# A second weight pool, other rooms and steps in the feed-forward block of a two-layer trunk

## The chip, the cores and the metric

The kernel runs on one core of a Trainium2 chip. The metric is the device time of one execution in microseconds (us). The core has five engines that run side by side, each through its own instructions in order: TensorE (PE in the profile, with its weight loads as PEld), VectorE (DVE), ScalarE (ACT), GpSimd (POOL) and SyncE (SP, which here only issues transfers). POOL and ACT issue transfers too; all transfers share 16 DMA engines. Engines wait for each other through semaphores.

## The reference, cut to what matters

The model is a trunk of two layers. Layer 0 is a gated linear attention, layer 1 a chunked softmax attention; each is followed by the same kind of feed-forward block (FFN). The change touches the FFN alone.

```python
D_MODEL, SEQ, FFN_DIM, FFN_CONV = 1024, 1024, 2816, 3

def conv_ffn(xn, w_up, conv_w, conv_b, w_down):
    h = causal_dwconv(xn @ w_up, conv_w) + conv_b     # 1024 x 5632, three taps along the sequence
    gate, val = h[..., :FFN_DIM], h[..., FFN_DIM:]
    return (jax.nn.silu(gate) * val) @ w_down         # back to 1024 x 1024

h = h + conv_ffn(rmsnorm(h, f_norm[layer]), f_w_up[layer], f_conv[layer], f_conv_b[layer], f_w_down[layer])
```

All of it is float32.

## The kernel before, in words

**Products of float32.** An operand of a product is cut in two: a high part (a cast to the matmul's type, on ACT or POOL) and a low part (operand minus high part, on POOL or DVE). A product is the sum of high x high, high x low and low x high, so three matmuls for each pair of tiles (`triple`). The cuts of the up-weights are called `uh`, `ul`, those of the down-weights `dh`, `dl`, those of the hidden channels (the down-product's other operand) `eh`, `el`.

**Tiles.** The 2816 hidden channels are 22 tiles `j` of 128. Both large products use a scheme of Strassen's kind: seven products of half size in the place of eight, with sums and differences of quarters of the operands. `product(j, n)`, n = 1 to 7, is one of the seven of the up-product of tile j (its gate and its value together); `second(g, n)` is one of the seven of the down-product of the pair g of hidden tiles, g = 0 to 8 for tiles 0 to 17; its products run in the order n = 1, 2, 5, 3, 6, 7, 4. Each is 12 matmuls. Tile 0 is done by eight plain products (`plain`), and tiles 18 to 21 by plain products at the end (`part` in layer 0, `tile_of` in layer 1), for which their hidden values are kept as cut tiles `hid` (function `hidden`).

**Order.** All products of a layer stand in one list `seq`, one step each. Everything else is a job, put at a step with `at(step, function, rank)`; the loop at the end runs, for each step, its jobs in order of rank and then its product. So the order of the instructions on every engine is written out by hand. A steady group is 21 steps: 14 up-products (two tiles) and 7 down-products.

**What stands where.** `load` brings a quarter of an up-weight (256 KB) into a room `r11`, `r12`, `r21` or `r22`. Those of tile 0 are issued by POOL, all others by SP. `operand` makes the sum that product n needs (DVE) and cuts it (ACT, then POOL, or DVE). `load_a` and `weights` do the same for the down-weights, with rooms `a11` to `a22` and `ay`; `channels` makes the channels' operand and its cut `e`. `drain` moves a down-product from PSUM into a staging tile on ACT or DVE; `send` adds it, as a transfer that accumulates (512 KB, issued by POOL), to one of four quarters of h in memory, `d_r` or, in layer 1, `d_c`. The first of the seven, n = 1, belongs to all four quarters: it is summed over the groups in two halves `d_e`, and at the end each half is read back (`load_e`) and sent three more times (`send_e`).

**Rooms.** Weights and cuts of the FFN lie in one pool `wf` at the right end of the on-chip memory; a tile waits for the last access to whatever lay at its address. Before the FFN, the residual's norm (lines 353 to 391: squares on ACT, their sum `nacc` on DVE, two small products `pss` and `psb` on PE, the scaling of h on DVE) uses the other free space. Eight slots h0 to h7 of the pool `hp` (1024 x 128 values each) hold, in turn, the values of four tiles (`val`, slots j mod 4), four staging tiles (h4 to h7), `hid` and the shared sum's halves. In layer 1 the slots have names with another number, and are used alike.

**End.** `load_last` loads the down-weights of tiles 18 to 21 (`fr`, into rooms of `wf`), `cut_last` cuts them (`fh`, `fl`); `load_r` (layer 1) loads what is to be added (`res`).

The lines of the profile that matter below: L1357 is every sum, difference and low cut of the FFN (`tt`; tiles tell which), L1377 the high cuts, L1389 to L1391 the matmuls of both products (tiles `pu` and `pd`), L1435 the loads of up-weights, L1472 to L1478 the convolution's taps, L1492 `hid`'s high part, L1710 and L1718 the sends, L1714 `load_e`, L1758 and L1764 the last tiles' weights and their cut.

Of the kernel before, what the change touches and what calls it, by code (L numbers as in the profile page):

```python
# [9 lines left out]
F32 = mybir.dt.float32  # L10
F32R = mybir.dt.float32r
# [5 lines left out]
P = 128  # L17
SEQ = 1024
KT = 8
HALF = 512  # L20
NH_A = 8
NH_B = 16
FP = 22
# [5 lines left out]
def trunk_kernel(  # L29
# [15 lines left out]
    nc = tc.nc  # L45
    SB = dict(reuse_waits="tile")
# [300 lines left out]
    hp = wp = None  # L347
# [157 lines left out]
    with ExitStack() as ph:  # L505
# [709 lines left out]
        h, late = [], None  # L1215
# [136 lines left out]
    def ffn(layer, h, hp, xs, tail, d_r, last):  # L1352
# [3 lines left out]
        sub, add = ALU.subtract, ALU.add  # L1356
# [4 lines left out]
        left, right = ExitStack(), ExitStack()  # L1361
        tp = left.enter_context(tc.tile_pool(name=f"ft{layer}", bufs=1, **SB))
        wf = right.enter_context(tc.tile_pool(name=f"fw{layer}", bufs=1, side="right", **SB))
        ctx_x = ExitStack()
        xt = ctx_x.enter_context(tc.tile_pool(name=f"xt{layer}", bufs=1, **SB))
        NG = 9
        RINGS = dict(u=3, d=2, e=2)
# [3 lines left out]
        def at(i, f, rank=1):  # L1371

            jobs.setdefault(max(i, 0), []).append((rank, f))

        def cut_high(src, ring, copy=nc.scalar.copy):
            hi, lo = [wf.tile([P, HALF], F32R, name=ring + x, tag=ring + x, bufs=RINGS[ring]) for x in "hl"]
            copy(hi, src)  # L1377
            return hi, lo

        def cut_low(src, hi, lo, eng):  # L1380
            tt(eng, lo, src, hi.bitcast(F32), sub)
# [45 lines left out]

        def room(j, q):
            tag = {(2, 12): "dh", (1, 21): "a21", (1, 22): "a22"}.get((j, q), f"r{q}")
            return wf.tile([P, 4, P], F32, name=f"r{q}", tag=tag, bufs=1 if tag == "r12" or tag[0] == "a" else 2)  # L1430

        def load(j, q, t_=None):
            t_ = t_ or room(j, q)
# [22 lines left out]
        pre, conv_t, hid, keep, bank = {}, {}, {}, {}, {}  # L1456
# [26 lines left out]
        def hidden(j, c0=0, c1=SEQ):  # L1483

            if j not in hid:
                if j == FP - 1:
                    hid[j] = [fin.tile([P, SEQ], F32R, name=f"hid{i}", tag=f"hid{i}") for i in "hl"]
                else:
                    room_ = {18: 6, 19: 4, 20: 2}[j]
                    hid[j] = [hp.tile([P, SEQ], F32R, name=f"hid{i}", tag=f"h{layer + 1}_{room_ + n}") for n, i in enumerate("hl")]  # L1490
            (hh, hl), v_ = hid[j], conv_t[j, 1]
            nc.scalar.copy(hh[:, c0:c1], v_[:, c0:c1])  # L1492
            tt(nc.vector, hl[:, c0:c1], v_[:, c0:c1], hh[:, c0:c1].bitcast(F32), sub)
# [29 lines left out]
        pos = {}  # L1523
# [34 lines left out]
        for c, (j, n) in enumerate(plan):  # L1558
# [3 lines left out]
            for g in range(NG):  # L1562
                for n, o in zip(ORDER, (2, 3, 5, 6, 8, 9, 11) if g == 0 else (-2, 0, 2, 4, 6, 8, 10)):
                    if c == 7 * (2 * g + 1) + 6 + o:
                        step(("d", g, n), lambda g=g, n=n: second(g, n))
        end = pos[FP - 1, 7]
        early = pos["p", 1, 3]
        for i, (j, n) in due.items():
            if i < early:
                low = []  # L1570
# [7 lines left out]
        def nx(j, s):  # L1578
            return pos[j + 1, s] if j + 1 < FP else end + s
# [23 lines left out]
        for j in range(3, FP - 1):  # L1603
# [4 lines left out]
        when = {  # L1608
            0: [(11, (g0,), 0), (12, (v0,), 0), (13, (v1,), 2), (13, (v2,), 2.7), (15, (g1, g2, silu), 2), (17, (gated,), 2)],
            1: [(18, (v0, v1), 2), (19, (v2, g0), 2), (20, (g1,), 2), (21, (g2, silu), 2), (22, (gated,), 2)],  # L1610
            2: [(24, (v0, v1), 2), (25, (v2, g0), 2), (26, (g1,), 2), (27, (g2, silu), 2), (28, (gated,), 2)],
        }
        for j in range(3, FP - 1):
            when[j] = [(pos[j, 7], (v0, v1), 2), (nx(j, 1), (v2, g0), 2), (nx(j, 2), (g1,), 2), (nx(j, 3), (g2, silu), 2), (nx(j, 4), (gated,), 2)]
            if j >= 2 * NG:
                when[j].append(({18: pos["d", NG - 1, 4] + 3, 19: pos["d", NG - 1, 4] + 7}.get(j, nx(j, 5)), (hidden,), 1.9))
        for j, w_ in when.items():
            for i, fs, r in w_:
                at(i, lambda j=j, fs=fs: [taps(j, *f) if isinstance(f, tuple) else f(j) for f in fs], r)
# [27 lines left out]
        araw, aops, bops, banks, stage = {}, {}, {}, {}, {}  # L1647

        def load_a(g, q):
            araw[g, q] = wf.tile([P, HALF], F32, name=f"a{q}", tag=f"a{q}", bufs=1)  # L1650
            nc.sync.dma_start(out=araw[g, q], in_=w_dn[(2 * g + q % 10 - 1) * P : (2 * g + q % 10) * P, hs(q // 10 - 1)])

        def weights(g, n):
            a = lambda q: araw[g, q]
            if n == 5:
                araw[g, 0] = wf.tile([P, HALF], F32, name="ay", tag="ay", bufs=1)
                tt(nc.vector, a(0), a(21), a(22), add)
            elif n == 3:
                tt(nc.vector, a(0), a(0), a(11), sub)
                tt(nc.vector, a(12), a(12), a(0), sub)  # L1660
            elif n == 7:
                tt(nc.vector, a(21), a(11), a(21), sub)
            aops[g, n] = cut(a({1: 11, 2: 12, 5: 0, 3: 12, 6: 0, 7: 21, 4: 22}[n]), "d")

        def channels(g, n):
            b11, b12, b21, b22 = [conv_t[2 * g + k, 1][:, hs(s)] for k in range(2) for s in range(2)]
            if n == 5:
                tt(nc.vector, b11, b12, b11, sub)
            elif n == 6:
                tt(nc.vector, b11, b22, b11, sub)  # L1670
            elif n == 7:
                tt(nc.vector, b12, b22, b12, sub)
            elif n == 4:
                tt(nc.vector, b21, b21, b11, sub)
            src = {1: b11, 2: b21, 5: b11, 3: b22, 6: b11, 7: b12, 4: b21}[n]
            bops[g, n] = cut_high(src, "e")
            cut_low(src, *bops[g, n], nc.gpsimd if n in (3, 6, 7) else nc.vector)

        def second(g, n):
            new = n in (1, 5, 6)  # L1680
# [18 lines left out]
        def total(n, u):  # L1699
            if n == 1:  # L1700
                return d_e[u]
            c, s = where[n]
            return d_c[c, s, u]
# [6 lines left out]
                    nc.gpsimd.dma_start(out=total(n, u), in_=stage[g, n, u], accum_op=add)  # L1710

        def load_e(u):
            stage["e", u] = hp.tile([P, SEQ], F32, name="stage", tag=f"h{layer + 1}_{4 + u}")
            nc.sync.dma_start(out=stage["e", u], in_=d_e[u])  # L1714

        def send_e(n):
            for u in range(2):
                nc.gpsimd.dma_start(out=total(n, u), in_=stage["e", u], accum_op=add)  # L1718

        for g in range(NG):  # L1720
            p_ = {n: pos["d", g, n] for n in ORDER}
            b_ = {n: pos["d", g - 1, n] for n in ORDER} if g else {1: p_[1] - 4, 3: p_[1] - 4, 7: p_[1] - 4, 4: p_[1] - 3}
            for q, n in ((11, 7), (12, 3), (21, 7), (22, 4)):
                at(b_[n] - 2, lambda g=g, q=q: load_a(g, q), 3 + q / 100)
            for n in ORDER:
                at(p_[n] - 3, lambda g=g, n=n: weights(g, n), 1.2)
                at(p_[n] - 3, lambda g=g, n=n: channels(g, n), 1.4)
                at(p_[n] + 1, lambda g=g, n=n: drain(g, n), 0)
                if n not in (3, 5):
                    at(p_[n] + 2, lambda g=g, n=n: send(g, n), 0.5)  # L1730
        fin_at = pos["d", NG - 1, 4]
        for u in range(2):
            at(pos["d", NG - 1, 7] + 3, lambda u=u: load_e(u), 3)
        for n, i in ((6, 4), (7, 5), (4, 6)):
            at(fin_at + i, lambda n=n: send_e(n), 0.5)


        k0 = 2 * NG
# [8 lines left out]

        def load_last(q):
            tag = ("a11", "a12", "r11", "r21", "r22", "r11", "r22", "r21")[q]
            bufs = 1 if tag[0] == "a" else 2  # L1750
            if layer == 0:
                t_ = wf.tile([P, 4, P], F32, name="fr", tag=tag, bufs=bufs)
                nc.sync.dma_start(out=t_, in_=w_dn[k0 * P :, q * P : (q + 1) * P].rearrange("(k p) m -> p k m", p=P))
                t_ = t_.rearrange("p k m -> p (k m)")
            else:
                k, c = q // 2, q % 2
                t_ = wf.tile([P, HALF], F32, name="fr", tag=tag, bufs=bufs)
                nc.sync.dma_start(out=t_, in_=w_dn[(k0 + k) * P : (k0 + k + 1) * P, hs(c)])  # L1758
            fw[q] = t_

# [68 lines left out]
        else:  # L1829
# [6 lines left out]
            res = {}  # L1836

            def load_r(t):

                for c in range(2):  # L1840
                    if t < 4:
                        tag = ("eh", "el", "dh", "dl")[t % 2 * 2 + c]
                        r_ = wf.tile([P, 4, P], F32, name="res", tag=tag, bufs=2)
                    else:
                        r_ = actp.tile([P, 4, P], F32, name="res", tag=f"x{'hl'[c]}{t}_1")
                    for u in range(2):
                        nc.sync.dma_start(out=r_[:, 2 * u : 2 * u + 2], in_=d_r[c, t // 4, u].rearrange("p (f t) -> p f t", f=2)[:, :, kc[t % 4]])
                    res[t, c] = r_
# [79 lines left out]
    with ExitStack() as ph:  # L1928
# [204 lines left out]
        h = []  # L2133
# [163 lines left out]
```

## Time and profile before

| what | value |
|---|---|
| median of 3 runs | 2687.33 us (2683.79 to 2688.33) |
| profiled execution | 2685.01 us, of which span 2683.3 us |
| mean granted clock of TensorE | 0.981 |
| TensorE busy | 2542.1 us, 95% of the span |
| VectorE, ScalarE, GpSimd busy | 67%, 53%, 56% |
| transfers | 326.71 MB, mean 122 GB/s |
| first FFN | about 680 to 1375 us of the span |
| second FFN | about 1966 us to the end |

A group of instructions is named by its line, its engine and `out<-in` with the names of the tiles. In a view of waits, a line tells which engine and line waited for which, the total in us, how many times, and the longest. In a timeline a line has the start, the length, what ran, and in brackets the idle time before it and what ended that. The chain of waits follows the work that ended last backwards, from what released each piece. Matmuls overlap: one that is listed with 0.39 us is followed by the next after 0.23 us.

### The profile page before, as it was taken

The numbers are of one execution on the slowest core, as the hardware profiler recorded it, in microseconds if no ns is written. First come the engines' busy times: TensorE is split into PE (matmuls) and PEld (weight loads), VectorE is DVE, ScalarE is ACT, GpSimd is POOL, SyncE is SP. The second block draws the span as 40 slices with busy tenths as digits, with TensorE's granted clock in tenths as the row PEclk, the third lists the DMA queues.
The fourth block names the chain that finished last, engine by engine and source line by source line (L and its number), as shares of the span: only waits on it lengthen the run. The fifth ranks groups of instructions, "written<-read, shape, count | busy, mean of one in ns | idle before, by whom it ended". The sixth has DMA issues, their size and how long they took to land.

```text
span 2683.3 us, 39404 instructions
## 1 busy us (share of the span) xinstructions
PE 2542.1 (95%) x13933; PEld 2083.7 (78%) x13933; DVE 1807.4 (67%) x3084; ACT 1410.3 (53%) x2714; POOL 1492.2 (56%) x1490
## 2 busy tenths in 40 slices
PE   7999999999899999999899999998979999999988
PEld 5888778888677888788678888887766788888767
DVE  5756765553678777877676666665468777778856
ACT  5444546563455555555355555555345555555633
POOL 3655543346257777777545444434243777777851
PEclk9999999999899999999899999999989999999989
DMA  4534435455237777767831111114222577777685
GB/s 129 137 102 118 121 117 158 138 172 170 59 82 152 150 153 144 144 130 141 200 117 50 50 47 42 50 40 147 88 87 75 134 149 144 151 154 143 133 184 173
DMA packets 317845, 326.71 MB, mean 122 GB/s; under 512 B 33232, under 2 KB 240848, under 8 KB 317648
## 3 DMA queue, kind: packets, MB, share of 16 engines
q1 hardware_dynamic: 286192, 219.07, 27.7%
q0 software_dynamic: 26560, 96.48, 20.4%
q10 hardware_dynamic: 4896, 8.65, 0.9%
q8 instruction: 109, 1.79, 0.3%
q14 instruction: 88, 0.72, 0.1%
HBM read 180.94 MB, written 143.20 MB: 121 GB/s over the span
## 4 chain that ended last, share of the span: by engine, by line
PE 40%; issue 8%; DVE 8%; POOL 7%; ACT 3%; DMA 3%; ACTq 0%; DVEq 0%; POOLq 0%
PE pu L1391 5%; PE pu L1390 4%; PE pu L1389 4%; PE acc L120 3%; PE acc L121 3%; POOL ul L1357 3%; PE acc L122 3%; PE pd L1391 2%; PE pd L1390 2%; PE pd L1389 2%; DVE r L1357 2%; DVE val L1475 2%; PE ptp L2047 2%; PE poT L2077 1%; ACT uh L1377 1%
## 5 line engine op out<-in xcount | busy, mean ns | idle before, releaser
L1357 POOL TENSOR_TENSOR ul<-r,uh 128x512 fp32r<-128x512 f32 x282 | 440.2, 1571 | 354.4 <-ACT uh L1377 331.7
L120 PE MATMUL acc<-xh,whi 128*128 128x512 f32 x896 | 376.2, 420 | 0.3 <-ACT xh L1096 0.2
L1377 ACT CAST uh<-r 128x512 fp32r<-128x512 f32 x296 | 179.7, 620 | 365.3 <-DVE r L1357 289.2
L121 PE MATMUL acc<-xl,whi 128*128 128x512 f32 x896 | 354.6, 396 | 1.6 <-POOL xl L379 1.0
L122 PE MATMUL acc<-xh,wlo 128*128 128x512 f32 x896 | 353.7, 395 | 0.6 <-POOL wlo L105 0.6
L105 POOL TENSOR_TENSOR wlo<-wraw,whi 128x256 fp32r<-128x256 f32 (+1 forms) x293 | 236.0, 836 | 204.7 <-ACT whi L103 162.8
L1389 PE MATMUL pu<-xh,uh 128*128 128x512 f32 x552 | 219.7, 398 | 25.8 <-POOL uh L1377 17.2
L1391 PE MATMUL pu<-xh,ul 128*128 128x512 f32 x552 | 219.1, 397 | 7.1 <-POOL ul L1357 7.0
L1390 PE MATMUL pu<-xl,uh 128*128 128x512 f32 x552 | 218.5, 396 | 1.0 <-POOL xl L379 1.0
L122 PEld LDWEIGHTS acc<-xh,wlo 128*128 128x128 f32 x896 | 169.4, 189 | 38.5 <-POOL wlo L105 1.0
L121 PEld LDWEIGHTS acc<-xl,whi 128*128 128x128 f32 x896 | 170.8, 191 | 26.2 <-POOL xl L379 3.1
L1357 DVE TENSOR_TENSOR r<-r,r 128x512 f32<-128x512 f32 x168 | 178.0, 1059 | 19.2 <-POOL ul L1357 19.1
L120 PEld LDWEIGHTS acc<-xh,whi 128*128 128x128 f32 x896 | 170.7, 191 | 23.3 <-ACT xh L1096 1.2
L1475 DVE SCALAR_TENSOR_TENSOR val<-vpre,colt,val 128x1023 f32<-128x1023 f32 (+2 forms) x92 | 154.3, 1677 | 39.3 <-ACT val L1472 39.2
L1695 ACT COPY stage<-pd 128x1024 f32<-128x1024 f32 x180 | 173.2, 1012 | 1.1 <-PE pd L1391 1.0
L1357 POOL TENSOR_TENSOR dl<-a,dh 128x512 fp32r<-128x512 f32 x90 | 160.5, 1784 | 20.5 <-ACT dh L1377 20.5
L2027 POOL TENSOR_SCALAR sS<-sS,st 128x640 f32<-128x640 f32 (+4 forms) x128 | 87.6, 688 | 143.6 <-DVE st L2026 124.4
L1389 PEld LDWEIGHTS pu<-xh,uh 128*128 128x128 f32 x552 | 105.7, 191 | 49.9 <-POOL uh L1377 18.1
L1475 DVE SCALAR_TENSOR_TENSOR gate<-gpre,colt,gate 128x1023 f32<-128x1023 f32 (+2 forms) x92 | 134.4, 1461 | 0.2
L2025 ACT ACTIVATE sS<-sS,st 128x640 f32<-128x640 f32 (+4 forms) x128 | 89.1, 696 | 83.2 <-DVE st L2024 83.0
L1391 PEld LDWEIGHTS pu<-xh,ul 128*128 128x128 f32 x552 | 105.5, 191 | 33.3 <-POOL ul L1357 11.4
L1357 DVE TENSOR_TENSOR el<-val,eh 128x512 fp32r<-128x512 f32 x72 | 68.0, 945 | 90.5 <-ACT eh L1377 90.5
(389 smaller groups left out, 7109.4 us busy)
## 6 DMA issues: line engine op xcount, KB each, us to landing
r<-in_f_w_up_dram SPq DMA_DIRECT2D x168, 256.0 KB, 4.3
d_r<-stage POOLq DMA_DIRECT2D x78, 512.0 KB, 7.6
d_c<-stage POOLq DMA_DIRECT2D x70, 512.0 KB, 8.0
a<-in_f_w_down_dram SPq DMA_DIRECT2D x72, 256.0 KB, 2.8
wraw<-in_a_w_in_dram SPq DMA_DIRECT2D x32, 512.0 KB, 4.6
d_e<-stage POOLq DMA_DIRECT2D x32, 512.0 KB, 9.3
wraw<-in_a_w_out_dram SPq DMA_DIRECT2D x16, 512.0 KB, 4.1
d_r<-h ACTq DMA_DIRECT2D x32, 256.0 KB, 2.7
```

What stands on the lines that cost most here:

```text
L105: nc.gpsimd.tensor_tensor(lo[:, c], raw[:, c], hi[:, c].bitcast(F32), op=ALU.subtract)
L120: mm(ps, hi[:, kw, wcol : wcol + P], rh[k][s], start=st, stop=False)
L121: mm(ps, hi[:, kw, wcol : wcol + P], rl[k][s], start=False, stop=False)
L122: mm(ps, lo[:, kw, wcol : wcol + P], rh[k][s], start=False, stop=sp)
L1357: tt = lambda eng, o, a, b, op: eng.tensor_tensor(o, a, b, op=op)
L1377: copy(hi, src)
L1389: mm(ps, w[0][:, cw], x[0], start=first, stop=False, skip_group_check=True)
L1390: mm(ps, w[0][:, cw], x[1], start=False, stop=False, skip_group_check=True)
L1391: mm(ps, w[1][:, cw], x[0], start=False, stop=last, skip_group_check=True)
L1475: nc.vector.scalar_tensor_tensor(t_[:, a:c1], p_[:, a - step : c1 - step], w[:, 2 - step : 3 - step], t_[:, a:c1], op0=ALU.mult, op1=ALU.add)
L1695: nc.scalar.copy(t_, ps)
L2025: nc.scalar.activation(S, S, AF.Exp, bias=st[:, 1:2], accum_out=st[:, 2:3])
```

## The change

Four things are edited.

1. The down-product's weights (`a11` to `a22`, `ay`), the channels' cuts (`eh`, `el`) and, at the end, the tiles that take over their rooms go to a pool `wd` of their own, which lies below `wf` on the right. What stays in `wf` thereby lies at higher addresses.
2. The hidden tiles 18, 19 and 20 go to slots (h5, h6), (h7, h2) and (h3, h4) instead of (h6, h7), (h4, h5) and (h2, h3); tile 18 is cut two steps later.
3. The shared sum: the first half is read back into h3 at the step of the last group's product 5, and sent two and three steps after it; the second half into h4, two steps after the last down-product, and sent two and three steps after that. Before, both were read back at one step, into h4 and h5, and each send was issued for both halves.
4. The channels' high cut comes ahead of the weights' work of the same step, and the low cut one step later. Of the low cuts, POOL makes those of products 5, 6 and 7 (before: 3, 6 and 7) and DVE the others.

```diff
@@ ffn
+        wd = right.enter_context(tc.tile_pool(name=f"fd{layer}", bufs=1, side="right", **SB))
...
         def cut_high(src, ring, copy=nc.scalar.copy):
-            hi, lo = [wf.tile([P, HALF], F32R, name=ring + x, tag=ring + x, bufs=RINGS[ring]) for x in "hl"]
+            hi, lo = [(wd if ring == "e" else wf).tile([P, HALF], F32R, name=ring + x, tag=ring + x, bufs=RINGS[ring]) for x in "hl"]
...
         def room(j, q):
             tag = {(2, 12): "dh", (1, 21): "a21", (1, 22): "a22"}.get((j, q), f"r{q}")
-            return wf.tile([P, 4, P], F32, name=f"r{q}", tag=tag, bufs=1 if tag == "r12" or tag[0] == "a" else 2)
+            return (wd if tag[0] == "a" else wf).tile([P, 4, P], F32, name=f"r{q}", tag=tag, bufs=1 if tag == "r12" or tag[0] == "a" else 2)
...
-                    room_ = {18: 6, 19: 4, 20: 2}[j]
-                    hid[j] = [hp.tile([P, SEQ], F32R, name=f"hid{i}", tag=f"h{layer + 1}_{room_ + n}") for n, i in enumerate("hl")]
+                    room_ = {18: (5, 6), 19: (7, 2), 20: (3, 4)}[j]
+                    hid[j] = [hp.tile([P, SEQ], F32R, name=f"hid{i}", tag=f"h{layer + 1}_{n}") for n, i in zip(room_, "hl")]
...
-        end = pos[FP - 1, 7]
+        end, fin_at = pos[FP - 1, 7], pos["d", NG - 1, 4]
...
-                when[j].append(({18: pos["d", NG - 1, 4] + 3, 19: pos["d", NG - 1, 4] + 7}.get(j, nx(j, 5)), (hidden,), 1.9))
+                when[j].append(({18: fin_at + 5, 19: fin_at + 7}.get(j, max(nx(j, 5), fin_at + 9)), (hidden,), 1.9))
...
         def channels(g, n):
...
             bops[g, n] = cut_high(src, "e")
-            cut_low(src, *bops[g, n], nc.gpsimd if n in (3, 6, 7) else nc.vector)
+            return lambda: cut_low(src, *bops[g, n], nc.gpsimd if n in (5, 6, 7) else nc.vector)
...
         def load_e(u):
-            stage["e", u] = hp.tile([P, SEQ], F32, name="stage", tag=f"h{layer + 1}_{4 + u}")
+            stage["e", u] = hp.tile([P, SEQ], F32, name="stage", tag=f"h{layer + 1}_{(3, 4)[u]}")
             nc.sync.dma_start(out=stage["e", u], in_=d_e[u])
 
-        def send_e(n):
-            for u in range(2):
-                nc.gpsimd.dma_start(out=total(n, u), in_=stage["e", u], accum_op=add)
+        def send_e(u, n):
+            nc.gpsimd.dma_start(out=total(n, u), in_=stage["e", u], accum_op=add)
...
                 at(p_[n] - 3, lambda g=g, n=n: weights(g, n), 1.2)
-                at(p_[n] - 3, lambda g=g, n=n: channels(g, n), 1.4)
+                low = []
+                at(p_[n] - 3, lambda g=g, n=n, low=low: low.append(channels(g, n)), 1.1)
+                at(p_[n] - 2, lambda low=low: low[0](), 1.1)
...
-        fin_at = pos["d", NG - 1, 4]
-        for u in range(2):
-            at(pos["d", NG - 1, 7] + 3, lambda u=u: load_e(u), 3)
-        for n, i in ((6, 4), (7, 5), (4, 6)):
-            at(fin_at + i, lambda n=n: send_e(n), 0.5)
+        for u, i in ((0, pos["d", NG - 1, 5]), (1, fin_at + 2)):
+            at(i, lambda u=u: load_e(u), 3)
+            for k, n in enumerate((6, 7, 4)):
+                at(i + 2 + k // 2, lambda u=u, n=n: send_e(u, n), 0.6)
```

In the same way `load_a`, `weights` (for `ay`), `load_last` (where its room is an `a`) and `load_r` (where it is `eh` or `el`) take their tiles from `wd`.

More of the change, by code (lines that the diff above doesn't have):

```diff
@@ L1649, in load_a @@
         def load_a(g, q):
-            araw[g, q] = wf.tile([P, HALF], F32, name=f"a{q}", tag=f"a{q}", bufs=1)
+            araw[g, q] = wd.tile([P, HALF], F32, name=f"a{q}", tag=f"a{q}", bufs=1)
             nc.sync.dma_start(out=araw[g, q], in_=w_dn[(2 * g + q % 10 - 1) * P : (2 * g + q % 10) * P, hs(q // 10 - 1)])
@@ L1655, in weights @@
             if n == 5:
-                araw[g, 0] = wf.tile([P, HALF], F32, name="ay", tag="ay", bufs=1)
+                araw[g, 0] = wd.tile([P, HALF], F32, name="ay", tag="ay", bufs=1)
                 tt(nc.vector, a(0), a(21), a(22), add)
@@ L1749, in load_last @@
             tag = ("a11", "a12", "r11", "r21", "r22", "r11", "r22", "r21")[q]
-            bufs = 1 if tag[0] == "a" else 2
+            wp_, bufs = (wd, 1) if tag[0] == "a" else (wf, 2)
             if layer == 0:
-                t_ = wf.tile([P, 4, P], F32, name="fr", tag=tag, bufs=bufs)
+                t_ = wp_.tile([P, 4, P], F32, name="fr", tag=tag, bufs=bufs)
                 nc.sync.dma_start(out=t_, in_=w_dn[k0 * P :, q * P : (q + 1) * P].rearrange("(k p) m -> p k m", p=P))
@@ L1756, in load_last @@
                 k, c = q // 2, q % 2
-                t_ = wf.tile([P, HALF], F32, name="fr", tag=tag, bufs=bufs)
+                t_ = wp_.tile([P, HALF], F32, name="fr", tag=tag, bufs=bufs)
                 nc.sync.dma_start(out=t_, in_=w_dn[(k0 + k) * P : (k0 + k + 1) * P, hs(c)])
@@ L1842, in load_r @@
                         tag = ("eh", "el", "dh", "dl")[t % 2 * 2 + c]
-                        r_ = wf.tile([P, 4, P], F32, name="res", tag=tag, bufs=2)
+                        r_ = (wd if tag[0] == "e" else wf).tile([P, 4, P], F32, name="res", tag=tag, bufs=2)
                     else:
```

## The prediction

> **What bounds the kernel now.** I read the page first, then what TensorE (PE) waits for in five stretches, then what the engine named there was itself waiting for.
>
> ```profile
> PE 2542.1 (95%) x13933; PEld 2083.7 (78%) x13933; DVE 1807.4 (67%) x3084; ACT 1410.3 (53%) x2714; POOL 1492.2 (56%) x1490
> ```
>
> PE is busy 95% of the span and the change leaves its 13,933 matmuls and their order alone. So a gain can come only from PE's holes and from the half clock behind them. The FFN's holes are these (waits of PE: start of the first FFN, start of the second, nine groups of the first, end of the first, end of the second):
>
> ```profile
> PE pu L1389 <- POOL uh L1377: 5.7, 1, 5.7
> PE pu L1391 <- POOL ul L1357: 2.8, 1, 2.8
> ...
> PE pu L1389 <- POOL uh L1377: 11.5, 1, 11.5
> PE pu L1391 <- POOL ul L1357: 1.4, 1, 1.4
> ...
> PE pd L1390 <- POOL el L1357: 6.6, 9, 1.1
> ...
> PE pu L1389 <- ACT uh L1377: 10.7, 2, 7.2
> ...
> PE pu L1389 <- ACT uh L1377: 13.0, 3, 6.8
> ```
>
> Behind the two starts stands POOL, which issues the first four loads of up-weights (waits of POOL, then the timeline of the first start, then the chain of waits of the second):
>
> ```profile
> POOL r L1435 <- DVE nacc L364: 8.1, 1, 8.1
> ...
> POOL r L1435 <- DVE nacc L367: 11.6, 1, 11.6
> ...
> 673.74 1.01 POOL L1435 DMA_DIRECT2D r<-in_f_w_up_dram  x1
> 682.83 2.25 POOL L1435 DMA_DIRECT2D r<-in_f_w_up_dram  x3 [8.09 <-DVE nacc L364]
> ...
> 1970.91 0.70 DVE nacc L367
> 1971.61 0.69 issue
> 1972.31 0.84 POOL r L1435
> 1973.15 5.04 DMA r<-in_f_w_up_dram
> 1978.24 0.61 POOL uh L1377
> ```
>
> The reader sees a weight load, which needs nothing that the norm computes, waiting for the norm's last sum: its room is memory that the norm's squares still occupy. The two ends show ACT held by a transfer, and the group the cut `el` of the fourth down-product (timelines of ACT, and of POOL in a group):
>
> ```profile
> 1294.04 1.05 ACT L1492 CAST hidh<-val 128x1024 fp32r<-128x1024 f32 x1 [4.58 <-DMA d_r<-stage]
> 1314.56 1.04 ACT L1492 CAST hidh<-val 128x1024 fp32r<-128x1024 f32 x1 [6.30 <-DMA d_r<-stage]
> ...
> 2607.32 0.62 ACT L1764 CAST fh<-fr 128x512 fp32r<-128x512 f32 x1 [10.19 <-DMA fr<-in_f_w_down_dram]
> ...
> 1074.98 1.68 POOL L1357 TENSOR_TENSOR ul<-r,uh 128x512 fp32r<-128x512 f32 x1 [1.34 <-ACT uh L1377]
> 1076.62 2.27 POOL L1357 TENSOR_TENSOR dl<-a,dh 128x512 fp32r<-128x512 f32 x1
> 1078.86 1.28 POOL L1357 TENSOR_TENSOR el<-val,eh 128x512 fp32r<-128x512 f32 x1
> ```
>
> The sum is made against the profiled execution: 2685.01 us, of which 2683.3 is span. The median of the three runs is 2687.33.
>
> **1. The second pool, at the first FFN.** It pushes the `r` rooms to other addresses: POOL's four loads no longer wait for the norm. POOL is free at 673.74 and the four issues take 1.01 + 2.25 us, so they are out by 677. The first needs 5 us to its cast (the chain's 5.04), so `uh` is done by 679.5 and its `ul` (3.72 for three, 1.24 each, behind two casts of 0.6) by 681.7. PE's first matmul must still wait until DVE has emptied the last output bank, at 680.8. Third matmul at 681.75 instead of 689.77; the hole before it is under 1.3 us, behind which no row shows half clock. The remaining ten matmuls take 0.227 us instead of 0.43: 684.0 instead of 694.2. The norm's sum, ready at 682.5, doesn't hold the matmuls `pss` that follow. Before, they and six more matmuls also ran at half clock (694.20 to 698.47); now 0.8 + 6 x 0.227 = 2.2 us, so `psb` starts at 686.2 instead of 698.47. All that follows hangs on `psb` (DVE scales h from it and is then 19.82 of 20 us busy from 700 to 720). Gain 12.3; I take 11.5, because the second `ul` and `dh` inherit the wait on the norm (a new wait at 682.5 with `ul` needed at 685.3: 1.24 us of work, so covered). Ends: 8 (only the two holes) and 12.3.
>
> **2. The same at the second FFN.** POOL is free at 1960.7; the loads go out then, 11.6 us earlier. `uh` by 1966, `ul` 2.5 us later at 1968.5, where it was 1980.1. Matmuls 3 to 24 at 0.227: 1973.5, where `pss` started at 1987.89. Its input is ready at 1971.6. Gain 14.4; eight writes of h, 256 KB each, are in flight beside these loads, and a hole of 2.5 us lies between those with and without half clock, so I take 13.5. Ends: 9 (landing 5 us later) and 14.4.
>
> **3. The groups.** 18 groups, nine per layer. The cut of the fourth product's low part goes from POOL to DVE and all low cuts go one step (2.72 us) after the high cut. On DVE `el` takes 0.945 in its row and DVE reaches it about 4 us before POOL did, so `dl`, then POOL's last, is out at about 1076.7, 2.4 us before PE's 1079.10. The wait of 0.70 costs 0.97 with the restart of the pipe (PE's next two matmuls start 1.09 and 0.34 after the one before, where 0.23 each is the pace), 0.74 in the second layer: 9 x 0.97 + 9 x 0.74 = 15.4, and 1.5 of small waits on `ul` in the same place: 17. In exchange the third product's `el` (1.28 on POOL alone, 1.98 with DVE beside it, by the spread of `ul`) is put ahead of an `ul` before which POOL idles 0.72 and that ends 0.4 before its use: from 0.2 us late (1.28 - 0.72 - 0.4) to 0.9 late. Ends: 17, and 17 - 18 x 0.9 = 1. I take 15, near the first, since the low cuts moved back a step leave POOL less crowded there. On DVE the two exchanged cuts balance. The weights' cuts `dh` now come after the channels' `eh` on ACT and so behind DVE's difference for it: 0.6 us, with two steps to spare.
>
> **4. End of the first FFN.** Hidden tile 18 goes to h5 and h6 two steps later, and no longer waits on ACT for the send that landed at 1296.68: hole 3.54 and its half clock (12 x 0.2 = 2.4) go. The same wait now stands on POOL, before the last of the shared sum's sends, ahead of an `ul`: POOL comes free at 1296.7, `ul` is out at 1298.9, PE wants it at 1299.5. Tile 19 in h7 and h2 no longer waits for sends landing at 1314.54 and 1317.36: hole 7.19 and 0.71 and 2.4 of half clock go. That is 16.2 of the 17.5 us by which this stretch exceeds its matmuls; DVE is next (21.85 of 40 us busy, but in a row of five dependent steps for the last tile), about 3 us. I take 13. On SP the load of the first shared half moves ahead of two `r` loads with 10 us to spare and waits for a send that landed at 1243.9; its three sends move ahead of `val` 19, which takes h3 some 3 us after I expect them landed. Ends: 8 and 15.
>
> **5. End of the second FFN.** The same holes, 4.26 with half clock, plus the load `fr` that took 13.7 us and held ACT until 2607.30. Three accumulating sends and one load leave this stretch for 30 us earlier. From the page, queue q0 took 20.4% of the span for 96.48 MB, so 512 KB cost 2.97 us of all 16 engines, and by q1 (27.7%, 219.07 MB) 1.8: 3 x 2.97 + 1.8 = 10.7 us less in front of `fr`, in a stretch whose DMA share is 1.08. `fr` lands at 2596.6, where PE without the first hole arrives at 2594.5: a hole of 3 stays instead of 6.83. With the smaller holes behind it, PE reaches the last tiles 11 us earlier. Ends: 5 (the transfers just come later) and 17.
>
> The Trainium skill ("TensorE: Matmul & The Clock Gate", Part 1) puts half rate behind an idle window of about 3.4 us, for about as long again. Here 16 matmuls in the first start and 12 after other holes ran at 0.43; by the page's figure each of five holes would cost 1.7 us in half clock instead of 2.4 to 3.6, and the sum an estimated 5 us less.
>
> **Sum.** 11.5 + 13.5 + 15 + 13 + 11 = 64. 2685.0 - 64 = 2621.
>
> **Rivals.**
> A. The ends only shift: sends of the shared sum hold POOL ahead of the last `ul`, and `fr` still waits in a full DMA. For it: share 1.08 there, and the landings of 9 to 15 us. Against it: 10.7 us of transfer leave the stretch. Parts 4 and 5 give 5 each, so 50: 2635.
> B. In the groups a new wait takes the old one's place, `ul` behind `el` on POOL, 0.9 late each time: part 3 gives 1, the sum 50, 2635; with A, 36, 2649. The Trainium skill ("GPSIMD Engine Reference", Key points) says that GpSimd shares its memory interfaces with VectorE and contends with VectorE's instructions of two inputs, as all these cuts are; that favours B. The trace agrees that they stretch (DVE's `r` 0.68 or 1.77 us).
> C. The pool moves nothing: the loads wait as before on another tenant of their new place. Then 25 of the sum go: 2646. Against it: the rooms now lie where the attention's tiles were, whose last use is long before 673 and 1960.
> D. Slower: POOL, in order, with `el` ahead of sends and `ul` in each of 18 groups. A wait over 3.5 us puts PE on half clock, 2.4 us more, so 6 a group: 108 lost against the 49 of the other parts, 2744. It decides from 49/18 = 2.7 us a group, when that `ul` comes 2 us later than the 0.9 above. POOL's 1.34 and 0.72 idle before two cuts speak against it.
>
> **How the numbers follow.** The forecast (sum 55 or more) 0.62; A or B alone 0.22; both, or C, 0.10; D 0.05; no change 0.01. Adding all low ends gives 31, all high ones 76. The range 2608 to 2652 holds the forecast, A, B, C and both A and B. Within 0.2% (5.4 us), about what a measurement can tell from no change: 0.01; faster 0.94; slower 0.05.
>
> **What would show it.** POOL's four loads issued together at about 674 and 1961, with no wait on `nacc`; `pss` at 684 and about 13 us before its old place in the second; no wait of PE's `pd` matmuls on POOL's `el`, and in B a new one on `ul` 18 times; `hidh` without a DMA before it; `fr` cast some 10 us after issue or less. Wrong if a load still waits, or if the waits on `ul` in the groups add up to over 15 us.

## The result

The changed kernel takes 2655.69 us (median of 4 runs, 2654.25 to 2659.89) beside 2687.17 us for the kernel before: a ratio of 0.9887, with a 95% interval of 0.987 to 0.9905. It is faster by 1.1%. The forecast was 2621 us with a range of 2608 to 2652; the direction was right, the size was twice what was measured, and the time lies 4 us above the range.

Since both kernels run the same 13,933 matmuls in one order, the n-th matmul of one can be set against the n-th of the other. The difference of their starts in the two profiled executions, and what each stretch adds to it (a steady group runs from the first matmul of its down-product n = 1 to that of the next group; the end begins behind the last down-product):

| stretch | forecast | measured |
|---|---|---|
| up to the first FFN | 0 | +1.0 |
| start of the first FFN (plain products and norm) | -11.5 | -10.9 |
| first group of the first FFN | (in the groups) | -4.8 |
| its eight steady groups | -15 for all | +12.3 |
| its end | -13 | -12.7 |
| its close and the second layer's attention | 0 | -0.2 |
| start of the second FFN | -13.5 | -13.1 |
| first group of the second FFN | (in the groups) | -3.1 |
| its eight steady groups | (in the -15) | +12.1 |
| its end | -11 | -11.1 |
| sum | -64 | -30.5 |

Four of the five parts came within 1 us. The groups were forecast to win 15 and lost 16. Single rows are known to about 2.5 us: beside the same trace of before, the first start is 2.5 us shorter in a kernel that leaves it alone (e11 below), and the second end 2.3 us shorter in one that leaves that alone (e3).

From the changed kernel, the page's line of busy time; PE's waits at the first start, at the second start, in the first FFN's steady groups, and at the two ends (lines of code are 1 to 2 higher than before):

```profile
PE 2533.4 (95%) x13933; PEld 2067.2 (78%) x13933; DVE 1907.7 (72%) x3084; ACT 1409.5 (53%) x2714; POOL 1483.6 (56%) x1490
...
PE pu L1392 <- POOL ul L1357: 1.4, 1, 1.4
PE pu L1390 <- DVE h L1258: 0.9, 1, 0.9
...
PE pu L1392 <- POOL ul L1357: 2.5, 1, 2.5
PE pss L370 <- DVE nacc L367: 0.3, 1, 0.3
...
PE pu L1392 <- POOL ul L1357: 5.6, 11, 0.7
PE pd L1391 <- POOL el L1357: 4.6, 7, 0.7
...
PE pu L1392 <- POOL ul L1357: 2.1, 2, 1.2
PE pu L1390 <- ACT uh L1378: 1.0, 2, 0.6
...
PE pu L1390 <- ACT uh L1378: 5.8, 3, 3.6
PE pu L1392 <- POOL ul L1357: 1.2, 2, 0.6
```

The holes of 5.7 and 11.5 us at the starts and of 7.2 and 6.8 at the ends are gone or halved. In the groups, where before one line stood (`pd` on `el`, 4.9 us in seven groups), there are two now, and VectorE is busy 100 us longer with as many instructions. Over the groups of both layers PE's waits on POOL's `el` stay as they were in sum (11.2 us in 18 waits before, 11.3 in 19 now), and those on POOL's `ul` go from 8.3 to 19.0 us. POOL's loads at the two starts, in the timelines of the changed kernel:

```profile
674.78 3.30 POOL L1436 DMA_DIRECT2D r<-in_f_w_up_dram  x4
679.09 0.61 POOL L1378 CAST uh<-r 128x512 fp32r<-128x512 f32 x1 [1.02 <-DMA r<-in_f_w_up_dram]
...
1945.45 3.13 POOL L1436 DMA_DIRECT2D r<-in_f_w_up_dram  x4
1949.27 0.62 POOL L1378 CAST uh<-r 128x512 fp32r<-128x512 f32 x1 [0.68 <-DMA r<-in_f_w_up_dram]
```

All four go out together and nothing of the norm stands before them. At the ends, ACT's timeline of the changed kernel has the hidden tiles without a wait, and `fr` with 4.34 instead of 10.19 us:

```profile
1295.42 1.05 ACT L1493 CAST hidh<-val 128x1024 fp32r<-128x1024 f32 x1
1301.43 1.04 ACT L1493 CAST hidh<-val 128x1024 fp32r<-128x1024 f32 x1
...
2576.80 0.62 ACT L1766 CAST fh<-fr 128x512 fp32r<-128x512 f32 x1 [4.34 <-DMA fr<-in_f_w_down_dram]
```

### The profile page after: what moved, and what is told of

The parts are those of the page before. It is cut to its first block, busy times and chain, and to the rows that moved or that the text cites. A ratio compares the mean times of both kernels' runs of the same rounds, so it can differ in the third digit from the quotient of the medians.

```text
span 2652.8 us, 39417 instructions
## 1 busy us (share of the span) xinstructions
PE 2533.4 (95%) x13933; PEld 2067.2 (78%) x13933; DVE 1907.7 (72%) x3084; ACT 1409.5 (53%) x2714; POOL 1483.6 (56%) x1490
## 5 line engine op out<-in xcount | busy, mean ns | idle before, releaser
L1357 DVE TENSOR_TENSOR r<-r,r 128x512 f32<-128x512 f32 x168 | 211.7, 1260 | 19.1 <-POOL ul L1357 19.0
L1476 DVE SCALAR_TENSOR_TENSOR val<-vpre,colt,val 128x1023 f32<-128x1023 f32 (+2 forms) x92 | 163.9, 1782 | 38.9 <-ACT val L1473 38.7
L1357 POOL TENSOR_TENSOR dl<-a,dh 128x512 fp32r<-128x512 f32 x90 | 144.2, 1602 | 28.9 <-ACT dh L1378 28.9
L1476 DVE SCALAR_TENSOR_TENSOR gate<-gpre,colt,gate 128x1023 f32<-128x1023 f32 (+2 forms) x92 | 150.6, 1637 | 0.2
L1357 DVE TENSOR_TENSOR el<-val,eh 128x512 fp32r<-128x512 f32 x72 | 102.0, 1417 | 36.2 <-ACT eh L1378 35.9
```

The source lines that it names most:

```text
L1357: tt = lambda eng, o, a, b, op: eng.tensor_tensor(o, a, b, op=op)
L1476: nc.vector.scalar_tensor_tensor(t_[:, a:c1], p_[:, a - step : c1 - step], w[:, 2 - step : 3 - step], t_[:, a:c1], op0=ALU.mult, op1=ALU.add)
```

## Where a steady group's 1.5 us come from

A steady group of 252 matmuls took 58.4 us before and takes 59.9 us. Matmul by matmul, averaged over six groups of the first FFN (g = 2 to 7), these are the only starts that come more than 0.3 us after the one before in one of the two kernels (full pace is 0.23). Products of the down-weights are named by their n, those of the up-weights by their tiles and by where they stand.

```
matmul that is late                      before   changed
pd<-el,dh    n=5, 2nd matmul              0.23     1.05
pu<-xt1h,ul  (two steps behind n=5)       0.23     0.40
pd<-el,dh    n=3, 2nd matmul              1.08     0.23
pd<-eh,dl    n=3, 3rd matmul              0.34     0.23
pu<-xh,ul    (step behind n=3)            0.23     1.01
pu<-xt1h,ul  (step behind n=4)            0.24     0.52
```

The wait that the change was to remove (n = 3) is gone. Four new ones stand for it.

## The experiments

Two theories at first. Theory 1: the order of the channels' low cuts in the queues makes the new waits. Theory 2: the second pool's addresses make VectorE and POOL slower, and the cuts are innocent.

**e1: the change without the channels' edit**

```diff
-                low = []
-                at(p_[n] - 3, lambda g=g, n=n, low=low: low.append(channels(g, n)), 1.1)
-                at(p_[n] - 2, lambda low=low: low[0](), 1.1)
+                at(p_[n] - 3, lambda g=g, n=n: channels(g, n), 1.4)
...
-            return lambda: cut_low(src, *bops[g, n], nc.gpsimd if n in (5, 6, 7) else nc.vector)
+            cut_low(src, *bops[g, n], nc.gpsimd if n in (3, 6, 7) else nc.vector)
```

> The changed kernel with the channels' cuts put back as before (high cut behind the weights' work, low cut in the same step, POOL for products 3, 6 and 7). Pool, hidden tiles and shared sum stay changed. Theory 1 (the queue order of the low cuts costs the groups their 1.5 us each): a steady group goes back from 59.9 to 58.4 us, 16 to 18 groups, so about 2630 us; starts and ends as in the changed kernel. Theory 2 (the new addresses of the second pool make VectorE's and GpSimd's instructions longer): a group stays at 59.9 and the time at about 2656 us.

Measured: 2640.64 us beside 2677.44 for the kernel before on this chip, ratio 0.986 (0.9838 to 0.9883). Groups of 58.4 us. Theory 2 falls, by the groups of the trace. The time is less good than 2630, the more so as the kernel before is 10 us faster on this chip than in the first result. Without the edit the first group of each layer also loses its gain of 3 us, so the channels' edit holds a gain and a loss; but that is not all of it. The four runs of this kernel lie 12 us apart (2633.91 to 2646.48), and the trace is of the fastest. Why they differ is open.

**e2: the channels' edit alone**, the diff of e1 the other way round, on the kernel before.

> The kernel before with the channels' cuts alone as in the change. Theory 1: groups of 59.9 us, the wait on el of product 3 gone and three new ones; about 25 us slower than before, 2712 us. Theory 2: groups of 57.5 us as the prediction's part 3 had it, about 2672 us.

Measured: 2696.40 us beside 2677.44, ratio 1.007 (1.0054 to 1.0087): 19 us slower. Groups of 59.9 us, and the first groups 3 us shorter in each layer. Theory 1 holds; the miss of 6 us is that first-group gain, which the expectation left out. Alone, this part of the change makes the kernel slower.

**e3: the second pool alone**

```diff
+        wd = right.enter_context(tc.tile_pool(name=f"fd{layer}", bufs=1, side="right", **SB))
...
-            hi, lo = [wf.tile(
+            hi, lo = [(wd if ring == "e" else wf).tile(
...
```

and the other tiles of `wd` as in the change, on the kernel before.

> The kernel before with the second pool alone. Theory 1: both starts as in the changed kernel, 10.9 + 13.2 us earlier, groups of 58.4 us, ends as before: about 2663 us. Theory 2: groups of 59.9 us, which eats the starts' gain: about 2688 us. If the first group's extra gain of 4 us in each layer belongs to the pool, 2655 us.

Measured: 2658.23 us beside 2677.44, ratio 0.9927 (0.9913 to 0.9942): 19 us faster. Groups of 58.4 us, no gain in the first group. PE's waits at the first and the second start, in this kernel:

```profile
PE pu L1392 <- POOL ul L1357: 1.5, 1, 1.5
PE pu L1390 <- DVE h L1258: 0.9, 1, 0.9
...
PE pu L1392 <- POOL ul L1357: 1.3, 1, 1.3
PE pss L370 <- DVE nacc L367: 1.1, 1, 1.1
```

These are the changed kernel's holes within a microsecond (2.4 in place of 2.8 us at the second start). The starts' gain belongs to the pool alone. By the trace it is 9.3 and 13.5 us, which is more than the 19 us that the runs on one chip show; the trace of before is from another chip.

**e4: high cut ahead, low cut at once**

```diff
-                low = []
-                at(p_[n] - 3, lambda g=g, n=n, low=low: low.append(channels(g, n)), 1.1)
-                at(p_[n] - 2, lambda low=low: low[0](), 1.1)
+                at(p_[n] - 3, lambda g=g, n=n: channels(g, n), 1.1)
...
-            return lambda: cut_low(src, *bops[g, n], nc.gpsimd if n in (5, 6, 7) else nc.vector)
+            cut_low(src, *bops[g, n], nc.gpsimd if n in (3, 6, 7) else nc.vector)
```

> The changed kernel with the channels' high cut ahead of the weights' work, as changed, but the low cut at once behind it, and on the engines of before (POOL for 3, 6 and 7). Theory 1: in the fourth product el now stands ahead of dl on POOL, and the wait of PE moves from el to dl, about 0.5 us instead of 0.8: groups of 58.1 us, about 2625 us. Theory 2: 2656 us, groups of 59.9.

Measured: 2662.05 us beside 2677.44, ratio 0.994 (0.9925 to 0.9955), groups of 59.7 us: a miss. The wait on `el` of n = 3 went and that on `dl` came (0.83 from start to start, as expected), but a new one of 1.09 came on a `ul` two steps before, and smaller ones on two more. So with the engines of before and no delay, merely putting the channels' cuts ahead of the weights' costs a group 1.3 us. Order alone is enough to lose nearly what the change loses.

Theory 1 was then split. 1a: the exchange of engines (product 5 to POOL, product 3 to VectorE) makes the new waits. 1b: being a step later does.

**e5: the changed kernel once more**, as a mark on the same chip.

> The changed kernel itself, beside the other kernels of this set on one chip. Every theory: about 31 us faster than before, steady groups of 59.9 us. It is the mark against which the next three are read.

Measured: 2652.77 us beside 2680.20, ratio 0.9896 (0.9881 to 0.9911), groups of 59.9 us.

**e6: a step later, engines as before**

```diff
-            return lambda: cut_low(src, *bops[g, n], nc.gpsimd if n in (5, 6, 7) else nc.vector)
+            return lambda: cut_low(src, *bops[g, n], nc.gpsimd if n in (3, 6, 7) else nc.vector)
```

> The changed kernel with the engines of the low cuts as before (POOL for products 3, 6 and 7) and the step later kept. Theory 1a (the exchange of engines makes the groups' new waits: el of product 5 on POOL behind dl, and el of product 3 on VectorE ahead of the gate's tap, whose silu holds ACT and so the next uh): the wait of 1.04 on el of product 5 and that of 1.01 on ul go, the wait of 1.08 on el of product 3 comes back, a group takes 58.4 to 58.9 us, and the first group keeps its gain of 3 us in each layer: about 18 us faster than the changed kernel. Theory 1b (being a step later makes them): groups stay at 59.9 us or get longer, at or above the changed kernel.

Measured: 2625.00 us beside 2680.20, ratio 0.9791 (0.9771 to 0.9811), 28 us faster than the changed kernel. Groups of 58.0 us. 1b falls. This kernel differs from e4 by the delay alone, and the delay is worth 1.7 us a group there (59.7 to 58.0); high cut ahead and delay together are worth 0.4 us a group over e1, and the first groups' gain besides. The changed kernel has that gain too and pays for the exchange.

**e7: the exchange alone**, as e1 but with POOL for 5, 6 and 7.

> The changed kernel with the channels' cuts at the place of before, behind the weights' work and in one step, but with the changed engines (POOL for 5, 6 and 7). Theory 1a: the two waits of the exchange are there without any delay of the cuts, groups of 59.5 to 59.9 us, and no gain in the first group: 5 us slower than the changed kernel to equal. Theory 1b: groups of 58.4 us or less, 16 us faster than the changed kernel.

Measured: 2670.96 us beside 2680.20, ratio 0.996 (0.9948 to 0.9973), 18 us slower than the changed kernel, groups of 60.5 us. 1a holds, and more strongly than expected. The exchange costs a group 2.1 us here (60.5 against e1's 58.4) and 1.9 us in the changed kernel (59.9 against e6's 58.0).

**e8: the cut of product 3 into POOL's idle time**

```diff
+                if g == 0:
+                    ...  # as changed
+                else:
+                    at(p_[n] - (4 if n == 3 else 3), lambda g=g, n=n: channels(g, n)(), 1.4)
...
-            ... nc.gpsimd if n in (5, 6, 7) else nc.vector)
+            ... nc.gpsimd if n in ((6, 7) if g == 0 else (3, 6, 7)) else nc.vector)
```

> Pool, hidden tiles and shared sum as changed. First group of each layer: high cut first and low cut a step later, POOL for products 6 and 7 alone. All other groups: cuts as before, but those of product 3 one step earlier, where POOL idles 1.3 us ahead of an ul. Theory 1a: the wait of 1.08 on el of product 3 goes and no new one comes, since POOL's work is only moved into its own idle time: groups of 57.4 us, first groups 4 us less: about 36 us faster than the changed kernel. If instead VectorE and POOL simply have no room for an earlier cut, the wait turns up at dl or ul: groups of 58.4 us, about 20 us faster than the changed kernel.

Measured: 2646.90 us beside 2680.20, ratio 0.9873 (0.9855 to 0.989), 6 us faster than the changed kernel: a miss of both. Groups of 59.4 us. The wait on `el` went, and waits of 0.94, 0.59 and 0.83 (start to start) came on three `ul`. POOL's idle 1.3 us was not free room. Beside the moved cut and the `ul` behind it, VectorE's two differences `ay` and `a` took 1.77 and 1.66 us where e1 has 0.68 and 0.69; ACT's `dh` came later by that, then its next `uh`, and POOL, which ran on without a pause at this place in e1, waits 1.67 us for that `uh`.

**e9 and e10: the exchange in halves.** In the changed kernel, POOL gets n = 3, 5, 6 and 7 (e9), or only 6 and 7 (e10).

> The changed kernel with POOL for the low cuts of products 3, 5, 6 and 7: half of the exchange, the cut of product 5 goes to POOL and that of product 3 stays there. Theory 1a by order (each wait belongs to one cut and its place in a queue): the wait of 1.04 on el of product 5 stays, that on el of product 3 stays at 0.96, that of 1.01 on ul goes: groups of 58.0 + 0.9 = 58.9 us, 16 us faster than the changed kernel. Theory 1a by sharing (VectorE is slower while POOL runs, and VectorE ends the chain to the next uh): more work on POOL in the same stretch lengthens VectorE's, the wait on ul stays as well: groups of 59.9 us or more.

> The changed kernel with POOL for the low cuts of products 6 and 7 only: the other half of the exchange, the cut of product 3 goes to VectorE and that of product 5 stays there. Theory 1a by order: el of product 3 on VectorE still stands ahead of the gate's tap, the wait of 1.01 on ul stays and takes the place of that on el: groups of 58.0 us, 28 us faster than the changed kernel. By sharing: POOL idles in that stretch and VectorE catches up, the wait on ul shrinks under 0.5: groups of 57.5 us, 36 us faster.

Measured: e9 2643.26 us beside 2680.82, ratio 0.9869 (0.9852 to 0.9885), groups of 59.2 us; e10 2633.56 us, ratio 0.9825 (0.981 to 0.9839), groups of 58.65 us. Averages over the same six groups:

```
matmul that is late                      e6     e9     e10    changed
pd<-el,dh    n=5, 2nd matmul            0.23   0.81   0.23    1.05
pu<-xt1h,ul  (two steps behind n=5)     0.23   0.40   0.23    0.40
pd<-el,dh    n=3, 2nd matmul            0.95   1.07   0.23    0.23
pd<-eh,dl    n=3, 3rd matmul            0.34   0.34   0.23    0.23
pu<-xh,ul    (step behind n=3)          0.23   0.23   1.03    1.01
pu<-xt1h,ul  (step behind n=4)          0.23   0.23   0.52    0.52
group, us                               58.0   59.2   58.65   59.9
```

Each wait belongs to one cut: those of rows 1 and 2 appear only where POOL cuts product 5, those of rows 5 and 6 only where VectorE cuts product 3. The halves cost 1.2 and 0.65 us, together 1.9, which is 59.9 - 58.0. The version by sharing is wrong in its forecast of the waits (the wait on `ul` neither stays in e9 nor shrinks in e10).

**e11: the ends alone**, that is the hidden tiles' slots and steps and the shared sum's steps, on the kernel before.

> The kernel before with the hidden tiles' slots and steps and the shared sum's steps alone as changed. If the ends are a gain of their own: 13 us at the first end and 10 at the second, groups of 58.4 us and starts as before, about 1 us lost in the last group of each layer where the first half is sent: 21 us faster than before. If they only pay because the other parts shift the transfers: under 10 us.

Measured: 2660.44 us beside 2680.82, ratio 0.9928 (0.9913 to 0.9942), 20 us faster; 9.4 and 10.2 us at the two ends by the trace, 0.9 lost in the last group of each layer. The ends are a gain of their own.

**e12: e6 with the low cut of product 3 ahead of `dl`**

```diff
-                at(p_[n] - 2, lambda low=low: low[0](), 1.1)
+                at(p_[n] - (3 if n == 3 else 2), lambda low=low: low[0](), 1.15)
```

> As the kernel with the step later and the engines of before, but the low cut of product 3 right behind its high cut and ahead of dl on POOL. The wait of 0.96 on el becomes one of about 0.7 on dl (the last of POOL's two cuts is the third matmul's, not the second's): groups of 57.8 us, 2 to 4 us faster than that kernel, 30 us faster than the changed one. By sharing: no gain, since the same work lies in the same stretch: within 2 us of that kernel.

Measured: 2625.07 us beside 2680.82, ratio 0.9799 (0.9779 to 0.9819); groups of 58.0 us as in e6. PE's late start moved from `el` (0.95) to `dl` (0.86), and in the second layer from `el` (0.84) to `dl` (0.96), whose matmul comes first there. No gain: what is short there is POOL's time for two cuts, whichever comes first.

The best kernel is e6, with e12 level: 1.0% below the changed kernel on the same chip (2625.00 against 2652.77). The medians of the parts do not add up: the pool gains 19 us (e3), the ends 20 (e11), the channels' edit loses 19 (e2), which makes 21, where the changed kernel gains 27 on its chip (e5). The 7 us between were not traced.

## How the exchange makes the waits

The timelines of POOL and then of VectorE over the same stretch, first in e6:

```profile
991.35 1.73 POOL L1357 TENSOR_TENSOR dl<-ay,dh 128x512 fp32r<-128x512 f32 x1
993.02 1.77 POOL L1711 DMA_DIRECT2D d_r<-stage  x2
995.50 1.61 POOL L1357 TENSOR_TENSOR ul<-r,uh 128x512 fp32r<-128x512 f32 x1 [0.71 <-ACT uh L1378]
...
990.37 1.57 DVE L1357 TENSOR_TENSOR el<-val,eh 128x512 fp32r<-128x512 f32 x1
...
994.69 1.27 DVE L1476 SCALAR_TENSOR_TENSOR gate<-gpre,colt,gate 128x1023 f32<-128x1023 f32 x1
995.88 1.78 DVE L1357 TENSOR_TENSOR r<-r,r 128x512 f32<-128x512 f32 x1
...
998.30 0.69 DVE L1357 TENSOR_TENSOR a<-a,ay 128x512 f32<-128x512 f32 x1
998.91 2.31 DVE L1476 SCALAR_TENSOR_TENSOR gate<-gpre,colt,gate 128x1022 f32<-128x1022 f32 x1
```

then in the changed kernel:

```profile
998.85 2.27 POOL L1357 TENSOR_TENSOR dl<-ay,dh 128x512 fp32r<-128x512 f32 x1
1001.09 1.72 POOL L1357 TENSOR_TENSOR el<-val,eh 128x512 fp32r<-128x512 f32 x1
1002.76 1.75 POOL L1711 DMA_DIRECT2D d_r<-stage  x2
1003.92 1.91 POOL L1357 TENSOR_TENSOR ul<-r,uh 128x512 fp32r<-128x512 f32 x1
...
1001.59 2.30 DVE L1476 SCALAR_TENSOR_TENSOR gate<-gpre,colt,gate 128x1023 f32<-128x1023 f32 x1
1003.82 2.57 DVE L1357 TENSOR_TENSOR r<-r,r 128x512 f32<-128x512 f32 x1
...
1007.02 0.69 DVE L1357 TENSOR_TENSOR a<-a,ay 128x512 f32<-128x512 f32 x1
1007.65 1.77 DVE L1357 TENSOR_TENSOR el<-val,eh 128x512 fp32r<-128x512 f32 x1
1009.34 2.31 DVE L1476 SCALAR_TENSOR_TENSOR gate<-gpre,colt,gate 128x1022 f32<-128x1022 f32 x1
```

*Product 5.* On POOL `el` stands behind `dl`, ends at 1002.8, and PE's second matmul of that product needs it: it starts 1.05 us behind the first. In e6 VectorE has it done at 991.9, before that `dl` ends (993.1).

*Product 3.* On VectorE `el` stands for 1.77 us between the weights' difference `a` and the gate's tap. Behind the tap is the silu, on ACT, and behind that in ACT's queue the casts `uh` of the next two up-products. ACT's timelines show it, first of the kernel before, where the silu and the casts follow ACT's own work without a wait, then of the changed kernel, where the silu waits for the tap:

```profile
1020.05 1.07 ACT L1478 ACTIVATE gate<-gate 128x1024 f32<-128x1024 f32 x1
1021.01 1.14 ACT L1377 CAST uh<-r 128x512 fp32r<-128x512 f32 x2
...
1011.74 1.06 ACT L1479 ACTIVATE gate<-gate 128x1024 f32<-128x1024 f32 x1 [1.54 <-DVE gate L1476]
1012.71 1.13 ACT L1378 CAST uh<-r 128x512 fp32r<-128x512 f32 x2
```

So POOL's `ul` comes late and PE waits at `pu<-xh,ul`. In this half (e10 against e6) a wait that costs 0.87 us with the matmul behind it was traded for one of 0.95 and 0.56 more at the two other `ul`.

## Why the prediction was wrong

*Parts 1 and 2 (the starts): right in mechanism and size.* The loads went out together, `pss` and `psb` followed. At the first start the second load landed 2.6 us behind the first, so the second `uh` came later than I had it: PE's hole before the third matmul was 1.4 us, and that matmul came 1.2 us later than worked out (the 1.0 us lost ahead of the FFN taken off). The 0.8 us that I had taken off for a wait on the norm cover more than half of this, but that wait (1.2 us, on ACT's `dh`) held no matmul; so far the size is luck. At the second start the hole was 2.5 us, as worked out, with no half clock behind it. Alone, the pool gave these holes too (e3).

*Part 4 (first end): right*, 12.7 against 13, with the send's wait on POOL covered as forecast: 1.43 us, after which POOL still waited for ACT's `uh`. The 2.1 us that PE waits there on two `ul` come from casts that follow VectorE's sums. *Part 5 (second end): right in size*, 11.1 against 11, but the time was won at another place than I had it. I had put 10.7 us less of transfers in front of `fr`; from issue to landing it took 12.7 us, hardly less than the 13.7 before. It was issued 10 us earlier against PE's arrival: before, SP spent 8.4 us on issuing the last load of `r` ahead of it, in the changed kernel 0.4. That the removed transfers are the cause is not shown. The hole behind `fr` fell from 6.8 to 1.6 us, where I had 3, and the next one grew from 1.9 to 3.6. Rival A fell; the ends alone give 20 us (e11).

*Part 3 (the groups): wrong, and in sign.* Forecast -15, measured -8 in the two first groups and +24 in the others; the waits on `ul` in the groups, which I had as a sign of being wrong above 15 us, add up to 19.0. Two steps of it failed, and a third held:

- "from 0.2 us late (1.28 - 0.72 - 0.4) to 0.9 late". I costed the `ul` that stands behind product 5's cut on POOL, but put the cut itself at nothing, and PE needs it at its second matmul (third in the second layer). That `ul` keeps PE's pace in the first layer; it is the cut that is late, by 0.8 us. The half of the exchange that moves it costs 1.2 us a group (e9 against e6).
- "On DVE the two exchanged cuts balance." They do in busy time, not in place: product 3's cut stands ahead of the tap that releases the silu and the next casts. The waits that come of it cost more than the one it removed, for which I had counted a gain of 0.97 us a group, 0.74 in the second layer; this half is worth +0.65 (e10 against e6).
- "since the low cuts moved back a step leave POOL less crowded" held: with the engines of before, the step later and the high cut ahead win 0.4 us a group (e6 against e1) and 3 to 4 us in the first groups, which I had not looked at.

*Rival B* had a new wait in the old one's place, but on the `ul` behind the cut and up to 0.9 us, which cancels the gain; what came are waits on the cut itself and behind VectorE's tap, and the exchange costs 1.9. Part 3 at +16 in place of -15 accounts for 31 of the 33.5 us between forecast and trace. *C* fell with e3. *D* did not come: the waits are about 1 us, without half clock in the steady groups.

The price was off too. I took `el` on VectorE at its mean of 0.945; in the changed kernel it took 1.77 where POOL's `ul` and `dl` run beside it, and the mean of all is 1.417.

## What to carry to other kernels

When a cut moves from one in-order queue to another, follow it in both: what needs its own result and when, and what stood behind its new place, through every engine, until it meets the bound engine again. Busy time that balances says nothing of that. Idle time on an engine is room only if using it doesn't slow the engine that it feeds: take the duration with the neighbour busy, and test an edit of several parts part by part, for here two good parts and half of a third carried a bad half that cost 28 us.

## What the runs showed of the hardware

The same VectorE instruction took very different times with the same operands: the gate's tap 1.27 us in e6, where POOL was idle for most of it, and 2.30 in the changed kernel, where POOL cut `el`; the sum `r` 1.78 and 2.57; POOL's `dl` 1.73 and 2.27. Over the whole kernel VectorE was busy 1807.4 us before, 1856.8 in e6 and 1907.7 in the changed kernel, with 3084 instructions each time. That the pairs which run together are the slow ones agrees with the Trainium skill ("GPSIMD Engine Reference", Key points: GpSimd shares its memory interfaces with VectorE, and contends with instructions of two inputs).

The traces show more: the sum `r` stood until POOL was done. With no sum, difference or cut of POOL beside it, `r` took 0.67 to 0.69 us every time (105 of them before, 93 in the changed kernel). Where `r` began while POOL had one under way, for another 0.1 us or more, and no further one followed beside it, `r` ended 0.55 to 0.56 us after POOL's, every time (42 before, 40 in e6, 22 in the changed kernel). In the lines above, `ul` of e6 ends at 997.11 and `r` at 997.66. How much of the 1.2 and 0.65 us a group is such waiting and how much is order was not separated.

Half clock did not follow from the length of the wait alone. At the close of the first FFN in the changed kernel, matmuls stood at 0.43 us from 1355.5 to 1356.8 (granted clock 0.50), shortly after a wait of 1.04 us at `pss`, and that stretch took 2.0 us longer than before; so it did in its second run (e5). Nine other kernels (e1, e2, e4, e6 to e10, e12) have this wait there or a longer one and kept the full pace. The other way round, in the first group the kernel before ran at half clock from 750 to 753 us, behind a wait of 1.7 us that every profile has; of the others only e8 shows it. So 1.6 of the 4.8 us won in the first group are no merit of the change. The prediction had taken holes under 1.3 us as free of half clock and one of 2.5 us as a doubtful case. Why it comes is open.
